# Sliding-window attention: probabilities and v in two rounded parts, v projected by features, on one Trainium2 core

## The chip, the cores and the metric

The kernel runs on one core of one Trainium2 chip. The metric is device time in microseconds. Before the change, three runs gave 2681.8, 2682.95 and 2688.42 us, with a median of 2682.95 us.

The engines are TensorE (PE, with PEld for its weight loads), VectorE (DVE), ScalarE (ACT), GpSimd (POOL) and SyncE (SP), which here only starts DMAs. Each engine works through its instructions in a fixed order, and an instruction that waits for another engine holds up everything behind it on its own engine.

## The reference

Four layers work on 16 meta tokens and 1024 sequence tokens with 1024 features. The layers are attention, mLSTM, HGRN2 and attention again. Only the two attention layers (the first and the last) matter here. They have 16 query heads in 4 groups; each group shares one key head and one value head of 64 features. A block of 128 queries sees its own block of keys and the one before it.

```python
def sliding_window_attention(q, k, v, sinks, valid):
    ...
    s = jnp.einsum('bnqhgd,bnkhd->bnhgqk', qb, kk) * (A_HD ** -0.5)
    ...
    s = jnp.where(mask[None, :, None, None], s, -jnp.inf)
    sink = sinks.astype(jnp.float32).reshape(A_KV, g, 1)
    m = jnp.maximum(s.max(axis=-1), sink)
    e = jnp.exp(s - m[..., None])
    p = e / (e.sum(axis=-1) + jnp.exp(sink - m))[..., None]
    o = jnp.einsum('bnhgqk,bnkhd->bnqhgd', p, vv)
    return o.reshape(bsz, lp, A_W)

def attention_branch(u, w_in, q_gain, k_gain, sinks, w_out, valid, pos):
    ...
    q = rope(rmsnorm(q.reshape(bsz, lp, A_HEADS, A_HD), q_gain), pos)
    k = rope(rmsnorm(k.reshape(bsz, lp, A_KV, A_HD), k_gain), pos)
    v = v.reshape(bsz, lp, A_KV, A_HD)
    o = sliding_window_attention(q, k, v, sinks, valid)
    return (o * jax.nn.silu(z.astype(jnp.float32))).astype(u.dtype) @ w_out
```

## The kernel before

**Number formats.** Everything is stored in float32. A product in F32 takes two instructions on PE, each of which passes over the moving columns. The large projections avoid this: `split` (L187) rounds an operand to F32R on ACT (the high part, suffix `h`) and takes the rest on DVE (the low part, suffix `l`), and three F32R products (high by high, high by low, low by high) are summed in PSUM, one instruction each. The profile writes both formats as f32; F32R outputs appear as fp32r.

**Layout.** The 1040 tokens are features by tokens, in three chunks of 400, 384 and 256 columns (`CHUNKS`). They form nine blocks: block 0 with the 16 meta tokens and blocks 1 to 8 with 128 each. `proj` (L238) computes 128 output features over a chunk with 24 products (L255), weights stationary. `proj_v` (L272) instead makes v with tokens as rows: for each block 24 products (L300) with u stationary and 256 value features moving. For the meta block the two parts of u lie side by side in the tile `um`, filled by GpSimd (L413), and 16 products (L296) suffice. The results go to the tiles `v`, 256 columns for all four value heads.

**The mixer.** For each of eight steps t, one PE tile of two query heads (hh = 0, 1) is processed. The blocks are grouped into units: block 0; blocks 1 and 2; 3; 4 and 5; 6; 7 and 8. For each unit there are three steps:

- `S_step` (L584): two F32R products per block give the scores in PSUM (L609, L610). POOL writes the sink beside them (L613), DVE adds the mask and finds the maximum (L614), ACT takes the exponential and its sum (L618), and DVE divides: reciprocal (L620) and a multiplication of 256 columns per block (L623).
- `T_step` (L625): PE turns the probabilities (L634, two transposes per block) into PSUM tile `pt`, and one ACT copy (L637 or L640) brings them to SBUF as `Pt`.
- `V_step` (L642): for each block two F32 products (L656), one with the previous block of v stationary and one with its own, over 128 query columns. Each product is two instructions. The stationary tile has the 128 features of two value heads, of which a query head needs 64. After the last unit of a chunk one ACT copy takes these 64 rows (L660).

In the last layer the meta block has no queries, so a layer has 96 or 80 units: 176 in all, of which 96 have two blocks, 64 have one, and 16 are the meta block.

**What sets the order.** PE's order is written by hand. `mixers` lists, for step k, the `V_step` of unit k − V_LAG, the `T_step` of unit k − T_LAG and the `S_step` of unit k, with planned costs; `weave` spreads these between the projections of the other heads in proportion to planned cost. ACT, DVE and POOL follow an order that a scheduler finds when the program is built, with raised priority for the mixer's steps. Weights arrive in halves of 128x512 through SP's queue and are split by ACT and DVE. All PSUM tiles rotate through eight buffers of one tag, v through ten, the small work tiles `t` through five.

**The stages.** The first layer's normalization and its k, v and first q projections run to 75 us; the eight steps t of the first attention layer run from there to 455 us; the mLSTM and the HGRN2 layer follow; the last attention layer has its steps t from 2252 us to the end. In t = 0, 6 and 7 there is least other work to weave in.

## Time and profile before

| | |
|---|---|
| runs | 2681.8, 2682.95, 2688.42 us |
| profiled execution: own time | 2687.3 us |
| profiled execution: span | 2685.5 us |
| mean granted TensorE clock | 0.994 |
| busy: PE, PEld, DVE, ACT, POOL | 2633.8, 2538.6, 1893.9, 1687.7, 154.2 us |

In the span's 40 equal slices, PE is at nine tenths or more in all but the first:

```profile
PE   7999999999999999999999999999999999999999
PEld 6999999999999999999999998999999899999999
DVE  6776777974747474747474688978878977677766
ACT  6767677555454545454545657877676857768673
POOL 1000000000000000000000000101000010000000
```

Slices 2 to 7 and the last seven are the attention layers. DVE and ACT are at six to eight tenths there.

### The profile page before, as it was taken

What the parts mean: (1) busy time and instruction counts of PE and PEld (TensorE: products, weight loads), DVE (VectorE), ACT (ScalarE), POOL (GpSimd) and SP (SyncE); (2) the same over time, 40 slices, a digit from 0 to 9 for tenths busy, and PEclk for the clock granted to TensorE, in tenths of its full rate; (3) what the DMA queues carried; (4) which work ended last, traced back from release to release, by engine and by line L of the source; (5) the groups of instructions that cost most, each with busy time, mean ns of one, the idle gap of its engine ahead of it and who ended that gap; (6) DMA issues with size and microseconds to landing.
All of it is one profiled execution on the core that took longest, in us unless ns stands there. A gap on an engine that the chain in (4) does not pass through costs nothing.

```text
span 2685.5 us, 55478 instructions
## 1 busy us (share of the span) xinstructions
PE 2633.8 (98%) x20896; PEld 2538.6 (95%) x20896; DVE 1893.9 (71%) x5335; ACT 1687.7 (63%) x4301; POOL 154.2 (6%) x545
## 2 busy tenths in 40 slices
PE   7999999999999999999999999999999999999999
PEld 6999999999999999999999998999999899999999
DVE  6776777974747474747474688978878977677766
ACT  6767677555454545454545657877676857768673
POOL 1000000000000000000000000101000010000000
PEclk9999999999999999999999999999999999999999
DMA  3211111011111111111111111111111111111102
GB/s 133 59 37 48 47 42 38 17 65 56 40 56 40 56 40 56 40 56 40 56 40 50 54 34 33 33 33 33 41 33 37 35 54 48 56 43 48 45 25 87
DMA packets 74044, 126.67 MB, mean 47 GB/s; under 512 B 11552, under 2 KB 26016, under 8 KB 73776
## 3 DMA queue, kind: packets, MB, share of 16 engines
q1 hardware_dynamic: 73776, 123.13, 14.4%
q8 instruction: 165, 2.70, 0.4%
q14 instruction: 103, 0.84, 0.1%
HBM read 108.24 MB, written 4.26 MB: 42 GB/s over the span
## 4 chain that ended last, share of the span: by engine, by line
PE 82%; DVE 10%; ACT 5%; DMA 1%; issue 1%; POOL 1%; SPq 0%; ACTq 0%; DVEq 0%; POOLq 0%
PE pj L255 38%; PE pj L338 15%; PE pj L300 10%; PE po L656 4%; PE pt L634 2%; PE po L862 1%; PE pm L609 1%; PE pa L532 1%; PE pa L876 1%; PE pm L610 1%; DVE t L408 1%; PE po L864 1%; DVE ul L189 1%; PE pj L296 1%; DVE x L341 1%
## 5 line engine op out<-in xcount | busy, mean ns | idle before, releaser
L255 PE MATMUL pj<-uh,wh 128*128 128x384 f32 (+2 forms) x2592 | 900.6, 347 | 3.8 <-ACT uh L188 3.8
L255 PE MATMUL pj<-ul,wh 128*128 128x384 f32 (+2 forms) x2592 | 836.5, 323 | 2.6 <-DVE ul L189 2.3
L255 PE MATMUL pj<-uh,wl 128*128 128x384 f32 (+2 forms) x2592 | 834.1, 322 | 0.1
L255 PEld LDWEIGHTS pj<-uh,wh 128*128 128x128 f32 x2592 | 492.0, 190 | 24.6 <-issue 6.6
L255 PEld LDWEIGHTS pj<-ul,wh 128*128 128x128 f32 x2592 | 492.6, 190 | 14.3 <-DVE ul L189 5.4
L255 PEld LDWEIGHTS pj<-uh,wl 128*128 128x128 f32 x2592 | 491.9, 190 | 0.4 <-DVE wl L189 0.4
L189 DVE TENSOR_TENSOR wl<-wr,wh 128x512 fp32r<-128x512 f32 x336 | 228.7, 688 | 59.6 <-ACT wh L188 56.6
L300 PE MATMUL pj<-wh,uh 128*128 128x256 f32 x896 | 270.1, 301 | 0.0
L188 ACT CAST wh<-wr 128x512 fp32r<-128x512 f32 x337 | 203.1, 618 | 96.9 <-PE pj L338 33.1
L341 DVE TENSOR_TENSOR x<-x,pj 128x384 f32<-128x384 f32 (+2 forms) x480 | 235.0, 510 | 39.7 <-PE pj L338 38.1
L338 PE MATMUL pj<-yh,wh 128*128 128x384 f32 (+2 forms) x768 | 254.0, 331 | 0.0
L300 PE MATMUL pj<-wh,ul 128*128 128x256 f32 x896 | 253.3, 283 | 0.0
L300 PE MATMUL pj<-wl,uh 128*128 128x256 f32 x896 | 253.3, 283 | 0.0
L338 PE MATMUL pj<-yl,wh 128*128 128x384 f32 (+2 forms) x768 | 246.8, 321 | 3.3 <-DVE yl L189 3.3
L338 PE MATMUL pj<-yh,wl 128*128 128x384 f32 (+2 forms) x768 | 246.0, 320 | 0.0
L428 DVE SCALAR_TENSOR_TENSOR t<-pj,t 128x384 f32<-128x384 f32 (+2 forms) x192 | 99.0, 515 | 110.4 <-ACT t L427 110.0
L618 ACT ACTIVATE Sm<-Sm,s 128x257 f32<-128x257 f32 (+2 forms) x272 | 131.7, 486 | 67.9 <-DVE s L614 65.8
L300 PEld LDWEIGHTS pj<-wl,uh 128*128 128x128 f32 x896 | 170.5, 190 | 2.2
L300 PEld LDWEIGHTS pj<-wh,uh 128*128 128x128 f32 x896 | 170.2, 190 | 2.5
L300 PEld LDWEIGHTS pj<-wh,ul 128*128 128x128 f32 x896 | 170.4, 190 | 0.0
L429 ACT ACTIVATE t<-t 128x384 f32<-128x384 f32 (+2 forms) x240 | 118.1, 492 | 81.0 <-DVE t L428 79.6
L614 DVE CUSTOM_DVE_ANT_0 Sm<-pm,masks,cons 128x256 f32<-128x256 f32 (+2 forms) x272 | 116.0, 452 | 70.0 <-PE pm L610 65.0
(218 smaller groups left out, 5290.0 us busy)
## 6 DMA issues: line engine op xcount, KB each, us to landing
wr<-in_b_win SPq DMA_DIRECT2D x128, 256.0 KB, 2.7
wr<-in_a_win SPq DMA_DIRECT2D x80, 256.0 KB, 2.7
wr<-in_c_win SPq DMA_DIRECT2D x64, 256.0 KB, 2.6
r<-rowsd SPq DMA_DIRECT2D x16, 520.0 KB, 5.8
wr<-in_a_wout SPq DMA_DIRECT2D x32, 256.0 KB, 2.7
wr<-in_b_wout SPq DMA_DIRECT2D x32, 256.0 KB, 2.7
t<-t SPq DMA_DIRECT2D x96, 48.0 KB, 1.9
wr<-in_c_wout SPq DMA_DIRECT2D x16, 256.0 KB, 2.7
```

The source lines that it names most:

```text
L188: s.copy(h, src)
L189: v.tensor_tensor(l, src, h.bitcast(F32), op=ALU.subtract)
L255: pe.matmul(acc[:, :cn], a[:, k, :], b[:, k, c0 : c0 + cn], start=(k == 0 and i == 0), stop=(k == KT - 1 and i == 2))
L300: pe.matmul(acc[:cn, :256], a[:, k, c0 : c0 + cn], m[:, kk, :], start=(k == 0 and i == 0), stop=(k == KT - 1 and i == 2))
L338: pe.matmul(acc[:, :cn], a[:, k, mc], b, start=(k == 0 and i == 0), stop=(k == 1 and i == 2))
L341: v.tensor_tensor(x[:, m, c0 : c0 + cn], x[:, m, c0 : c0 + cn], acc[:, :cn], op=ALU.add)
L428: v.scalar_tensor_tensor(a[:, :cn], z, 0.0, a[:, :cn], op0=ALU.min, op1=ALU.subtract)
L429: s.activation(a[:, :cn], a[:, :cn], AF.Exp)
L614: v.tensor_tensor_reduce(Sm[:nq, u, :nk], S[:nq, u, :nk], R["masks"][:nq, P + mo : P + mo + nk], -1.0, sink, ALU.add, ALU.min, st[:nq, u : ...
L618: s.activation(Sm[:nq, u, : nk + 1], Sm[:nq, u, : nk + 1], AF.Exp, scale=-1.0, bias=st[:nq, u : u + 1], accum_out=den[:nq, u : u + 1])
L634: pe.transpose(pt[:kn, u, ki, :nq], Sm[:nq, u, ko : ko + kn], ident[:nq, :nq])
L656: pe.matmul(po[:, q0 - c0 : q0 - c0 + nq], V[kb][:kn, gcol : gcol + P], Pt[:kn, u, ki, :nq], start=(ki == 0), stop=(ki == len(kbs) - 1))
```

## The change

The product of probabilities and v is made with F32R instead of F32.

- **v by features.** `v_proj` projects 128 value features (two value heads) with `proj`, as q and k are. The result is copied to SBUF, turned on PE (a transpose per block), and split into a high and a low part, which lie as [high head 0, low head 0, low head 1, high head 1] in 256 columns, so that 128 columns hold both parts of one head. The first two heads are projected in the head of the layer, the other two in the fill of t = 4. The meta tile `um` is no longer filled for attention layers, and has 48 columns instead of 80.
- **Probabilities in two parts.** `T_step` leaves the high part `Ph` (ACT) and the low part `Pl` (DVE). `Pl` has one buffer.
- **V_step.** Both parts pass over the stationary v of one head, [high, low] side by side, into the same 128 rows of PSUM; in a unit of two blocks the block that serves both queries is passed with 256 columns. The two halves of the rows are added: an ACT copy of one and a DVE addition of the other. V_LAG goes from 4 to 3.
- **Division.** The multiplication by the reciprocal moves from DVE to GpSimd.

```diff
-T_LAG, V_LAG = 2, 4
+T_LAG, V_LAG = 2, 3
+D_V = 1500.0
...
-                if n == 0:
-                    for z, src in ((0, uh), (64, ul)):
+                if n == 0 and self.meta:
+                    for z, src in ((0, uh), (32, ul)):
                         g.tensor_copy(um[:, k, z : z + NMETA], src[:, k, :NMETA].bitcast(F32))
...
+        def v_proj(src, jj):
+            late = {}
+            def evac(acc, n, c0, cn):
+                late[n] = tmp()
+                s.copy(late[n][:, :cn], acc[:, :cn])
+            def finish(n, c0, cn):
+                def fn():
+                    pt = psum("pt", 1)
+                    for k, b in enumerate(CHUNK_BLOCKS[n]):
+                        q0, nq = blk(b)
+                        pe.transpose(pt[:nq, P * k : P * k + P], late[n][:, q0 - c0 : q0 - c0 + nq], ident)
+                    for k, b in enumerate(CHUNK_BLOCKS[n]):
...
+                        parts = z[:nq, :256].rearrange("p (a c) -> p a c", a=4)
+                        src = pt[:nq, P * k : P * k + P].rearrange("p (a c) -> p a c", a=2)
+                        s.copy(parts[:, 0:4:3], src)
+                        v.tensor_tensor(parts[:, 1:3], src, parts[:, 0:4:3].bitcast(F32), op=ALU.subtract)
...
+            return proj(src, evac), [finish(n, *c) for n, c in enumerate(CHUNKS)]
...
-                    v.tensor_scalar(Sm[:nq, u, :nk], Sm[:nq, u, :nk], den[:nq, u : u + 1], None, op0=ALU.mult)
+                    g.tensor_scalar(Sm[:nq, u, :nk], Sm[:nq, u, :nk], den[:nq, u : u + 1], None, op0=ALU.mult)
...
-                w["Pt"] = Pt = R["mix"].tile([P, 2, 2, P], F32, tag="Pt", name=nm("Pt"), bufs=2)
+                w["Ph"] = Ph = R["mix"].tile([P, 2, 2, P], F32R, tag="Ph", name=nm("Ph"), bufs=2)
+                w["Pl"] = Pl = R["mix"].tile([P, 2, 2, P], F32R, tag="Pl", name=nm("Pl"), bufs=1)
...
+                s.copy(h, src)
+                v.tensor_tensor(l, src, h.bitcast(F32), op=ALU.subtract)
...
+                    runs = [(b, P, P * (2 * k + 1), 2 * P if k + 1 < len(unit) else P, P * k) for k, b in enumerate(unit)]
+                    runs.insert(1, (b0 - 1, P, 0, P, 0))
+                for i, (kb, kn, p0, w_, q0) in enumerate(runs):
+                    for part in ("Ph", "Pl"):
+                        flat_p = w[part].rearrange("p u k q -> p (u k q)")
+                        pe.matmul(po[:, a0 + q0 : a0 + q0 + w_], V[t // 4, kb][:kn, P * hh : P * hh + P],
+                                  flat_p[:kn, p0 : p0 + w_], start=(i == 0 and part == "Ph"),
+                                  stop=(i == len(runs) - 1 and part == "Pl"))
                 if w["last"]:
...
+                    s.copy(o, po[hs, :cn])
+                    v.tensor_tensor(o, o, po[os, :cn], op=ALU.add)
...
-                for lag, cost, fn in ((V_LAG, 427, V_step), (T_LAG, 213, T_step), (0, 218, S_step)):
+                for lag, cost, fn in ((V_LAG, 260, V_step), (T_LAG, 213, T_step), (0, 218, S_step)):
...
-        vg = proj_v(win[2], win[3], v_evac)
+        vg0, vfin0 = v_proj(win[2], 0)
+        vg1, vfin1 = v_proj(win[3], 1)
...
+            if t == 4:
+                parts.append(tile_of(vg1, vfin1))
```

The instructions of PE around one unit, in the first attention layer at t = 7, blocks 4 and 5, hh = 0. Before, its transposes and what follows at once (Sm holds the probabilities, pt their transposes, pm the scores of a later unit, po the output, pj a projection):

```order
L656 MATMUL po_5356<-Pt_5414,v_423 128x128
L634 MATMUL pt_5494<-const,Sm_5429 128x128 x4
L609 MATMUL pm_5501<-r_2857,qs_5107 128x256
L610 MATMUL pm_5501<-kl_2858,qs_5107 128x256
L656 MATMUL po_5383<-Pt_5456,v_381 128x128
L656 MATMUL po_5383<-Pt_5456,v_423 128x128
L255 MATMUL pj_5515<-uh,wh_5041 128x256
```

After these come five more projection products, and then the next unit's transposes and scores ahead of this unit's own products with v, which read Pt_5495:

```order
L634 MATMUL pt_5522<-const,Sm_5461 128x128 x4
L609 MATMUL pm_5529<-r_2859,qs_5110 128x256
L610 MATMUL pm_5529<-kl_2860,qs_5110 128x256
L656 MATMUL po_5540<-Pt_5495,v_423 128x128
L656 MATMUL po_5540<-Pt_5495,v_523 128x128 x2
L656 MATMUL po_5540<-Pt_5495,v_573 128x128
```

With the change, the same unit's transposes (L660) are followed by two score products (L634, L635) and then at once by its own products with v (L687):

```order
L687 MATMUL po_5716<-Pl_5832,v_3499 128x128
L660 MATMUL pt_5874<-const,Sm_5802 128x128 x4
L634 MATMUL pm_5883<-r_2879,qs_5449 128x256
L635 MATMUL pm_5883<-kl_2880,qs_5449 128x256
L687 MATMUL po_5894<-Ph_5875,v_3581 128x256
L687 MATMUL po_5894<-Pl_5876,v_3581 128x256
L687 MATMUL po_5894<-Ph_5875,v_3502 128x128
L687 MATMUL po_5894<-Pl_5876,v_3502 128x128
L687 MATMUL po_5894<-Ph_5875,v_3584 128x128
L687 MATMUL po_5894<-Pl_5876,v_3584 128x128
```

What moved: the transposes and the products that use them had the other unit's work and six projection products between them; now they have two score products. The eight instructions of the product (four F32 products of two) are six.

On DVE near the same place, before (ISA is the masked maximum and the reading of its result):

```order
L620 RECIPROCAL s_5463<-s_5463 128x2
L623 TENSOR_SCALAR Sm_5461<-Sm_5461,s_5463 128x256 x2
L614 ISA Sm_5502,s_5503<-pm_5501,masks_220,cons_222 128x256
L614 ISA s_5503 128x1
L620 RECIPROCAL s_5504<-s_5504 128x1
L623 TENSOR_SCALAR Sm_5502<-Sm_5502,s_5504 128x256
```

and with the change:

```order
L645 RECIPROCAL s_5840<-s_5840 128x2
L639 ISA Sm_5884,s_5885<-pm_5883,masks_194,cons_196 128x256
L639 ISA s_5885 128x1
L694 TENSOR_TENSOR r_5675<-r_5675,po_5716 64x400
L666 TENSOR_TENSOR Pl_5876<-pt_5874,Ph_5875 128x512
L645 RECIPROCAL s_5886<-s_5886 128x1
```

The multiplications are gone. The low part of the probabilities stands behind the next masked maximum and behind the addition that ends the chunk of another unit.

On POOL at the beginning of the mixer, with the change (before, only the L613 copies stood here, now L638):

```order
L638 COPY Sm_689<-cons_196 16x1
L638 COPY Sm_707<-cons_196 16x1
L648 ISA
L648 TENSOR_SCALAR Sm_689<-Sm_689,s_691 16x16
L638 COPY Sm_730<-cons_196 128x1 x2
L648 TENSOR_SCALAR Sm_707<-Sm_707,s_709 16x16
L638 COPY Sm_791<-cons_196 128x1 x2
L648 TENSOR_SCALAR Sm_730<-Sm_730,s_732 128x144
L648 TENSOR_SCALAR Sm_730<-Sm_730,s_732 128x256
```

The sink copy of a later unit now stands behind or ahead of the multiplications, which wait for DVE's reciprocals; one ISA instruction stands ahead of the first multiplication.

More of the change, by code (lines that the diff above doesn't have):

```diff
@@ L166, in hybrid_kernel @@
     ul = cpool.tile([P, KT, T], F32R, name="ul")
-    um = cpool.tile([P, KT, 80], F32R, name="um")
+    um = cpool.tile([P, KT, 48], F32R, name="um")
     g.memset(um.bitcast(F32), 0.0)
@@ L634, in T_step @@
                         pe.transpose(pt[:kn, u, ki, :nq], Sm[:nq, u, ko : ko + kn], ident[:nq, :nq])
[L635 to L640 removed]
+                if unit[0] == 0:
+                    src, h, l = (z[:NMETA, 0, 0, :nq] for z in (pt, Ph, Pl))
+                else:
+                    src, h, l = (z[:, :nu] for z in (pt, Ph, Pl))
+                s.copy(h, src)
+                v.tensor_tensor(l, src, h.bitcast(F32), op=ALU.subtract)
             def V_step(w):
[L643 removed]
+                unit, geo, hh, n, t = w["unit"], w["geo"], w["hh"], w["n"], w["t"]
                 nq = blk(unit[0])[1]
```

52 lines of the change are left out of this document (24 added, 28 removed).

## The prediction

> **What bounds the kernel now.** I read the page first, then the stretches of 20 us, then who waits for whom.
>
> ```profile
> span 2685.5 us, 55478 instructions
> PE 2633.8 (98%) x20896; PEld 2538.6 (95%) x20896; DVE 1893.9 (71%) x5335; ACT 1687.7 (63%) x4301; POOL 154.2 (6%) x545
> ...
> PE 82%; DVE 10%; ACT 5%; DMA 1%; issue 1%; POOL 1%; SPq 0%; ACTq 0%; DVEq 0%; POOLq 0%
> ```
>
> PE is busy for 98% of the span and makes 82% of the chain that ended last. The change touches only the two attention layers, so I look there. The columns are the stretch, its length, the busy time and count of PE, PEld, DVE, ACT and POOL, then granted clock and DMA:
>
> ```profile
> 320.00:340.00 20.00, 20.00 (x150) 19.51 (x149) 12.71 (x41) 10.48 (x29) 2.30 (x8) 1.00 0.19 59
> ...
> 400.00:420.00 20.00, 20.00 (x154) 19.48 (x152) 15.13 (x54) 16.82 (x49) 2.05 (x10) 1.00 0.01 2
> 420.00:440.00 20.00, 19.14 (x147) 18.38 (x146) 13.07 (x53) 16.19 (x47) 2.07 (x12) 1.00 0.01 2
> ```
>
> PE has hardly any idle time even in t = 7 (414 to 455 us), where ACT is busy for 16.8 of 20 us. PE's waits in the mixer are few, and those for the operands of L656 are nearly none:
>
> ```profile
> PE pt L634 <- DVE Sm L623: 3.1, 4, 1.4
> ...
> PE po L656 <- ACT v L270: 0.7, 1, 0.7
> ```
>
> So PE's order is the bound: work taken from PE is time gained, and each new wait on PE is time lost.
>
> **Products with v.** Starts of successive instructions give their price.
>
> ```profile
> 103.61 0.28 PE L255 MATMUL pj<-uh,wh 128*128 128x256 f32 x1
> 103.73 0.28 PE L255 MATMUL pj<-ul,wh 128*128 128x256 f32 x1
> ...
> 104.31 1.05 PE L656 MATMUL po<-Pt,v 128*128 128x128 f32 x8
> ...
> 69.14 2.85 PE pj L300 x24
> ...
> L656 PE MATMUL po<-Pt,v 128*128 128x128 f32 x1024 | 140.8, 275 | 0.7 <-ACT v L270 0.7
> L634 PE MATMUL pt<-const,Sm 128*128 128x128 f32 x512 | 82.5, 273 | 3.9 <-DVE Sm L623 3.1 <-ACT r L660 0.8
> ```
>
> An F32R product over 256 columns takes 0.119 us: two start 0.12 us apart, and 24 in the chain of waits take 2.85 us. An F32 instruction over 128 columns takes (1.05 − 0.275)/7 = 0.111 us. Before: 1024 × 0.111 = 113.7 us. After: the 96 units of two blocks have two products over 256 columns each, 192 × 0.119 = 22.8 us, and all 160 units have four over 128 columns, 640 in all. With p us for one of those, PE saves 90.9 − 640p. No row shows an F32R product over 128 columns. Half of the 256-column one is p = 0.06; the F32 product over the same columns is two instructions, p = 0.222. Between them lies the weight load, since every product here loads its own 128 columns:
>
> ```profile
> 83.21 0.29 PEld L656 LDWEIGHTS po<-Pt,v 16*128 16x128 f32 x2
> 83.22 0.39 PE L656 MATMUL po<-Pt,v 16*128 16x16 f32 x2
> ...
> L656 PE MATMUL po<-Pt,v x1056: 257/275/377, 83.2 to 2633.9; 128*128 128x128 f32 x171, 16*128 16x16 f32 x5
> L609 PEld LDWEIGHTS pm<-r,qs x272: 93/188/329, 75.2 to 2621.7; 128*128 128x128 f32 x128, 128*16 128x16 f32 x8
> ```
>
> Two products of only 16 moving columns still start 0.39 − 0.257 = 0.13 us apart, and their loads 0.29 − 0.19 = 0.10 us. An F32R load takes 188 ns for 128 columns and 93 for 16: the load, not the width, sets the pace of a narrow product. I take p = 0.111, nearest to the rows with 128 weights; 0.10 to 0.13 would save 27 to 8 us. **PE saves 19.9 us**, all of it in the units of two blocks; a unit of one block keeps four instructions of the same price.
>
> The Trainium skill, page "TensorE: Matmul & The Clock Gate", section "Back-to-back issue gap", speaks for more: it measured 81 ns for pairs of load and product at 128 columns. By it PE would save 39 us, and the forecast below would become 2678 us; the pair above, 0.10 to 0.13 us apart, does not agree with it.
>
> **v by features.** Before, 16 + 192 products over 256 columns a layer: 416 × 0.119 = 49.5 us in both.
>
> ```profile
> 108.25 0.34 PE L255 MATMUL pj<-uh,wh 128*128 128x400 f32 x1
> 108.43 0.34 PE L255 MATMUL pj<-ul,wh 128*128 128x400 f32 x1
> 108.61 0.35 PE L255 MATMUL pj<-uh,wl 128*128 128x400 f32 x1
> ...
> 108.80 0.60 PE L634 MATMUL pt<-const,Sm 128*128 128x128 f32 x4
> ...
> 109.77 0.58 ACT L640 COPY Pt<-pt 128x512 f32<-128x512 f32 x1
> ```
>
> After, 96 products in each chunk: 0.18 us for 400 columns, 0.173 in proportion for 384, and 0.119, so 96 × 0.472 = 45.3 us, and 36 transposes at (0.60 − 0.273)/3 = 0.109 us, 3.9 us. **Sum −0.3 us.** Half the projection, 12 us, leaves the head of the first layer, where PE is not always the bound, for t = 4, where it is:
>
> ```profile
> 40.00:50.00 10.00, 8.66 (x55) 7.69 (x55) 9.42 (x21) 8.79 (x22) 0.00 (x0) 1.00 0.08 21
> 50.00:60.00 10.00, 9.80 (x70) 8.49 (x69) 8.07 (x20) 6.96 (x19) 0.00 (x0) 1.00 0.01 2
> 60.00:70.00 10.00, 10.00 (x58) 9.65 (x58) 4.56 (x11) 8.84 (x20) 0.00 (x0) 1.00 0.29 86
> ```
>
> From 60 us on PE alone is full, so removing work there shortens the head; around 45 us DVE is (9.4 of 10), and PE could idle. The products that waited for `um` there are gone too. I set this term to 0, between −3 and +9 us.
>
> **The new wait.** This is the term that decides. Before, between a unit's last transpose and its first product with v lay more than a whole round of other work; with V_LAG 3 there is less than one, and now two steps must fit in instead of one: the ACT copy `Ph`, then DVE's `Pl`.
>
> ```profile
> L640 ACT COPY Pt<-pt 128x512 f32<-128x512 f32 x96 | 56.0, 583 | 13.2 <-PE pt L634 11.4 <-PE pm L610 0.8
> L640 ACT COPY Pt<-pt 128x256 f32<-128x256 f32 x64 | 23.5, 366 | 11.8 <-PE pt L634 11.5
> L189 DVE TENSOR_TENSOR wl<-wr,wh 128x512 fp32r<-128x512 f32 x336 | 228.7, 688 | 59.6 <-ACT wh L188 56.6
> L189 DVE TENSOR_TENSOR ul<-t,uh 128x256 fp32r<-128x256 f32 x32 | 13.1, 421 | 0.8 <-ACT uh L188 0.6
> ```
>
> With nothing in the way, a unit of two blocks needs, after its last transpose's turn on PE, 0.16 us until that transpose ends (0.273 − 0.109), 0.58 for the copy, 0.69 for the low part and 0.12 for the handovers: 1.56 us. (The 0.12 is an estimate: here DVE starts 0.03 us after ACT's end, which comes twice, and PE has to begin again.)
>
> ```profile
> 100.54 0.55 ACT L355 ACTIVATE t<-t 128x400 f32<-128x400 f32 x1
> ...
> 101.12 0.57 DVE L540 TENSOR_TENSOR t<-t,t 128x400 f32<-128x400 f32 x1 [0.98 <-ACT t L355]
> ```
>
> A unit of one block needs 0.16 + 0.37 + 0.42 + 0.12 = 1.08 us. In the place shown in the change, two score products stand between, 0.24 us: PE must wait for 1.3 us, and behind that product everything on PE waits too: transposes and scores of the next units and the projection.
>
> I priced the products between, with the numbers above, for all 160 units of the changed order. Of them 40 have less than 1.5 us and 88 less than 2 us; in the order before, none has less than 2 us. The shortfalls sum to 19 us if nothing is queued before the two steps. Something is: the copies started 0.37 us after the last transpose's end in the row above (108.80 + 0.60 to 109.77), and here 0.22 us:
>
> ```profile
> 105.92 0.38 PE L634 MATMUL pt<-const,Sm 128*128 128x128 f32 x2
> ...
> 106.52 0.37 ACT L640 COPY Pt<-pt 128x256 f32<-128x256 f32 x1
> ```
>
> With 0.3 us of queueing for both engines together the shortfalls sum to 34.5 us, with 0.6 us to 55, with 0.9 us to 83. I take 0.3 us, near the smaller of the two, since a PE that waits lets ACT and DVE catch up: **+34.5 us**, most of it in t = 0, 5, 6 and 7 of the first layer and t = 7 of the last.
>
> **DVE, ACT and POOL.** DVE loses the multiplications and gains the low parts and the closing additions.
>
> ```profile
> L623 DVE TENSOR_SCALAR Sm<-Sm,s 128x256 f32<-128x256 f32 x224 | 73.3, 351 | 3.0
> L613 POOL COPY Sm<-cons x272: 175/186/1304, 25.2 to 2621.9; 128x1 f32<-128x1 f32 x128, 16x1 f32<-16x1 f32 x8
> L613 POOL COPY Sm<-cons 128x1 f32<-128x1 f32 x256 | 57.4, 249 | 734.0 <-PE pt L634 362.4 <-ACT Sm L618 72.1 <-ACT t L355 32.4
> L1135 POOL COPY att<-rd 32x64 f32<-32x64 f32 x128 | 53.9, 421 | 507.2 <-DVE rd L1133 501.7
> ```
>
> The low parts are 96 × 0.69 + 64 × 0.42 = 93 us, about what the multiplications took, so DVE keeps its 13 to 15 of 20 us, with some 50 us more for 96 closing additions (0.5 us each, an estimate from the 0.42 and 0.69 above) over the 830 us of both layers. POOL's multiplication over 256 columns has no row. Its copies take 0.19 us for one column and 0.42 for 64, so it lies between DVE's 0.35 and, with 3.6 ns a column, 1.1 us; I take 0.45. That is 0.1 us a block and a handover longer than before, in a path from scores to transposes that has two rounds and gains two waits of PE: I cost it at nothing. If POOL takes 1.1 us, it adds about 1.5 us a unit to that path, and the dense units wait for it. The ISA row in front of it has no price in the trace; it stands behind copies that ran from 25.2 us on, and the first scores come at 75.2 us, so 50 us cover it.
>
> A rule speaks against this move: by the Trainium skill, page "SBUF — State Buffer", section "SBUF: two separate sides", GpSimd and a DVE instruction with two SBUF inputs exclude each other for a whole instruction. The longest sink copy above, 1304 ns against a median of 186, agrees. If each of the 256 long multiplications lost what the mean of those copies is above their median (249 − 186 ns), all of it on PE's path, the sum would be 16 us higher.
>
> **Sum.** 2687.3 (the profiled execution's own time) − 19.9 − 0.3 + 0 + 34.5 = 2701.6 us. The median of the runs, 2682.95, lies 4.35 us below that execution, so I forecast 2697 us.
>
> **Rivals.**
> - *Narrow products run at their width* (p = 0.06). For it: wide F32R products cost in proportion to columns. Against it: the pair of 16 columns. PE saves 52.5 us instead of 19.9: 2664 us, faster. It beats the waits of 34.5 us from p below 0.088.
> - *The F32R product over 128 columns is as slow as F32* (p = 0.222): the halving does not happen. No row excludes it. PE loses 51 us: 2768 us.
> - *The two steps are not late*: shortfalls between 0 and the floor of 19 us, because the scheduler places them first. 2663 to 2682 us. Against it: L694 and L639 stand ahead of L666 in DVE's order.
> - *Everything on ACT, DVE and POOL queues up* (0.9 us a unit, ACT being at 16.8 of 20): 2745 us.
>
> **How the numbers follow.** A measurement of this kernel can tell about 0.3% (8 us) from no change. Forecast 0.48 (own range 2680 to 2722: slower 0.38, same 0.10); products at their width 0.17 (faster 0.13, same 0.04); as slow as F32 0.12 (slower); steps not late 0.13 (faster 0.07, same 0.06); queueing 0.10 (slower). Faster 0.20, same 0.20, slower 0.60. The range from 2661 to 2756 leaves out the F32 case and the ends of the others.
>
> **What would show it.** The spacing of the narrow L687 rows gives p. L687 should appear among PE's waits for DVE `Pl`, with some 30 us, and PE's idle time in t = 0, 6 and 7 should rise from nearly 0 to 1 to 2 us in 20. The transposes L660 should not wait for POOL more than L634 waited for DVE. The first scores should come some 10 us earlier than 75.2 us. The forecast is wrong if p is far from 0.111, or if L687 hardly waits.

## The result, and the profile after

| | before | after |
|---|---|---|
| median of the runs | 2682.38 us (2679.79 to 2688.42, 4 runs) | 2755.64 us (2754.68 to 2759.61, 4 runs) |
| profiled execution, own time | 2687.3 us | 2759.6 us |
| ratio | | 1.0269, 95% interval 1.0251 to 1.0287 |

The kernel became 73 us slower. The forecast was 14 us slower.

The page of the changed kernel, with the rows that answer to those of before (span, busy time, the slices of PE and of POOL, the chain of work that ended last):

```profile
span 2757.8 us, 55198 instructions
...
PE 2649.7 (96%) x20612; PEld 2532.5 (92%) x20612; DVE 1968.0 (71%) x5369; ACT 1693.9 (61%) x4331; POOL 379.2 (14%) x787
...
PE   6899998999999999999999999999999998999999
...
POOL 0433244100000000000000000101000102332340
...
PE 70%; DVE 14%; ACT 8%; DMA 3%; issue 3%; POOL 1%; SPq 1%; DVEq 0%; ACTq 0%; POOLq 0%
```

PE's share of the chain falls from 82% to 70%, DVE's and ACT's rise from 15 to 22% together. PE's idle time, span less busy time, rises from 51.7 to 108.1 us. PE has 284 instructions fewer, yet 16 us more busy time: a product that starts after a pause is shown longer, as the rows of one unit will show, and work at half the clock, some 14 us more than before by the table below, counts as busy. A stretch of t = 6 in the first layer now (the columns are those of the stretches above):

```profile
420.00:440.00 20.00, 17.71 (x119) 16.14 (x118) 16.59 (x47) 14.85 (x42) 9.21 (x17) 1.00 0.12 34
```

Before, PE had no idle time in t = 6; now it has 2.3 of 20 us, with DVE at 16.6. Who PE waits for (total us, times, longest):

```profile
PE po L687 <- DVE Pl L666: 30.9, 53, 2.1
...
PE po L687 <- ACT Ph L665: 13.3, 23, 1.7
...
PE pt L660 <- POOL Sm L648: 5.5, 8, 1.3
```

The wait is where the prediction put it. Its size has to be read from starts, since this view counts only time in which PE was empty. For each pair of neighbouring PE instructions (line and form of both) I took the lower quartile of the time from start to start, over the traces of all runs shown here. The sum of these is called *work*. What a spacing has beyond it, if over 40 ns, is *lost*: to the instruction that came late, or to *half clock* where it began in a stretch of half the granted clock without idle time ahead. In us of each profiled execution:

| | work | of it P·v | lost at products with v | lost at transposes | half clock | all else | first to last PE start |
|---|---|---|---|---|---|---|---|
| before | 2460.0 | 114.9 | 2.7 | 5.4 | 14.6 | 190.3 | 2673.0 |
| after | 2444.6 | 96.5 | 78.6 | 6.4 | 28.9 | 186.5 | 2745.0 |
| difference | −15.4 | −18.4 | +75.9 | +1.0 | +14.3 | −3.8 | +72.0 |

The price of a narrow product with v in this count is 0.11 us. In the changed kernel 130 of the 640 started only 0.06 us after the one ahead, most of them the second narrow product behind wide ones, so PE saved some 7 us more than the 18.4; the count has that under "all else". The 79 us are in 192 places, spread over the dense stages: 6.5, 7.0, 6.0, 6.3 and 9.7 us in t = 0, 1, 5, 6, 7 of the first layer, 8.7 and 9.9 in t = 3 and 7 of the last.

One unit of t = 5 shows how. First PE, then ACT, then DVE in the timeline (start, duration, engine, line, operation, and in brackets the idle time ahead and who ended it):

```profile
380.73 0.60 PE L660 MATMUL pt<-const,Sm 128*128 128x128 f32 x4
...
382.34 0.28 PE L635 MATMUL pm<-kl,qs 128*128 128x256 f32 x1
383.13 0.38 PE L687 MATMUL po<-Ph,v 128*128 128x256 f32 x1 [0.51 <-ACT Ph L665]
383.86 0.38 PE L687 MATMUL po<-Pl,v 128*128 128x256 f32 x1 [0.34 <-DVE Pl L666]
384.08 0.22 PE L687 MATMUL po<-Ph,v 128*128 128x128 f32 x1
384.14 0.27 PE L687 MATMUL po<-Pl,v 128*128 128x128 f32 x1
384.25 0.27 PE L687 MATMUL po<-Ph,v 128*128 128x128 f32 x1
...
381.58 0.49 ACT L693 COPY r<-po 64x400 f32<-64x400 f32 x1
382.10 0.50 ACT L427 ACTIVATE t<-pj 128x400 f32<-128x400 f32 x1
382.50 0.58 ACT L665 CAST Ph<-pt 128x512 fp32r<-128x512 f32 x1
...
383.11 0.69 DVE L666 TENSOR_TENSOR Pl<-pt,Ph 128x512 fp32r<-128x512 f32 x1 [0.44 <-ACT Ph L665]
```

The transposes end at 381.33, but `Ph` begins at 382.50: ACT first takes another unit's closing copy and a piece of the gate. PE comes to the product at about 382.46 (382.34 and the usual 0.12), and starts it at 383.13. Then it waits for `Pl` too. The two products start 0.73 us apart, and the next one 0.22 us later, where without a wait each takes 0.12. PE loses 0.67 + 0.61 + 0.10 = 1.4 us here, of which the view of waits counts 0.85.

### The profile page after: what moved, and what is told of

The parts are those of the page before. It is cut to its first block, busy times and chain, and to the rows that moved or that the text cites. A ratio compares the mean times of both kernels' runs of the same rounds, so it can differ in the third digit from the quotient of the medians.

```text
span 2757.8 us, 55198 instructions
## 1 busy us (share of the span) xinstructions
PE 2649.7 (96%) x20612; PEld 2532.5 (92%) x20612; DVE 1968.0 (71%) x5369; ACT 1693.9 (61%) x4331; POOL 379.2 (14%) x787
## 4 chain that ended last, share of the span: by engine, by line
PE 70%; DVE 14%; ACT 8%; DMA 3%; issue 3%; POOL 1%; SPq 1%; DVEq 0%; ACTq 0%; POOLq 0%
PE pj L256 33%; PE pj L339 14%; PE pj L301 9%; PE po L687 2%; ACT Sm L643 1%; DMA t<-t 1%; PE pt L660 1%; DVE Pl L666 1%; PE po L901 1%; DVE t L410 1%; PE pa L915 1%; DVE ul L190 1%; PE po L903 1%; SPq L526 1%; DVE wl L190 1%
## 5 line engine op out<-in xcount | busy, mean ns | idle before, releaser
L256 PE MATMUL pj<-uh,wh 128*128 128x384 f32 (+2 forms) x2688 | 932.9, 347 | 4.6 <-ACT uh L189 4.6
L256 PE MATMUL pj<-ul,wh 128*128 128x384 f32 (+2 forms) x2688 | 870.9, 324 | 3.6 <-DVE ul L190 3.5
L256 PE MATMUL pj<-uh,wl 128*128 128x384 f32 (+2 forms) x2688 | 868.2, 323 | 0.0
L256 PEld LDWEIGHTS pj<-ul,wh 128*128 128x128 f32 x2688 | 513.7, 191 | 14.8 <-DVE ul L190 6.6
L648 POOL TENSOR_SCALAR Sm<-Sm,s 128x256 f32<-128x256 f32 (+2 forms) x272 | 252.4, 937 | 523.3 <-DVE s L645 509.4
L339 PE MATMUL pj<-yh,wh 128*128 128x384 f32 (+2 forms) x768 | 252.2, 328 | 0.0
L339 PE MATMUL pj<-yl,wh 128*128 128x384 f32 (+2 forms) x768 | 246.9, 321 | 3.2 <-DVE yl L190 3.2
L339 PE MATMUL pj<-yh,wl 128*128 128x384 f32 (+2 forms) x768 | 246.0, 320 | 0.0
L301 PE MATMUL pj<-wh,uh 128*128 128x256 f32 x768 | 231.3, 301 | 0.0
L301 PE MATMUL pj<-wh,ul 128*128 128x256 f32 x768 | 216.6, 282 | 0.0
L301 PE MATMUL pj<-wl,uh 128*128 128x256 f32 x768 | 216.5, 282 | 0.0
L189 ACT CAST yh<-r 128x384 fp32r<-128x384 f32 (+2 forms) x120 | 57.2, 479 | 152.1 <-PE pj L339 130.6
L339 PEld LDWEIGHTS pj<-yl,wh 128*128 128x128 f32 x768 | 144.7, 188 | 5.8 <-DVE yl L190 5.2
L301 PEld LDWEIGHTS pj<-wh,uh 128*128 128x128 f32 x768 | 145.2, 189 | 2.1
```

Of the source, the lines that this page charges most:

```text
L189: s.copy(h, src)
L256: pe.matmul(acc[:, :cn], a[:, k, :], b[:, k, c0 : c0 + cn], start=(k == 0 and i == 0), stop=(k == KT - 1 and i == 2))
L301: pe.matmul(acc[:cn, :256], a[:, k, c0 : c0 + cn], m[:, kk, :], start=(k == 0 and i == 0), stop=(k == KT - 1 and i == 2))
L339: pe.matmul(acc[:, :cn], a[:, k, mc], b, start=(k == 0 and i == 0), stop=(k == 1 and i == 2))
L648: g.tensor_scalar(Sm[:nq, u, :nk], Sm[:nq, u, :nk], den[:nq, u : u + 1], None, op0=ALU.mult)
```

## The experiments

Lost times are those of the table above, worked out in the same way from each run's trace. P·v stands for the products with v.

The column of half clock varies by itself: in the mLSTM and HGRN2 layers, where nothing was changed, it is between 6 and 17 us over these executions, so a difference of a few us in it tells nothing of an edit.

| run | median us | ratio to before (95%) | lost at P·v | at transposes | half clock |
|---|---|---|---|---|---|
| the change | 2755.6 | 1.0269 (1.0251 to 1.0287) | 78.6 | 6.4 | 28.9 |
| e1_control | 2800.3 | 1.0443 (1.0428 to 1.0459) | 76.7 | 6.4 | 30.6 |
| e1_lag4 | 2764.0 | 1.0308 (1.0292 to 1.0323) | 5.2 | 40.3 | 27.2 |
| e2_high_only | 2723.7 | 1.0158 (1.0141 to 1.0175) | 48.6 | 8.7 | 22.6 |
| e2_high_only_lag4 | 2701.1 | 1.0074 (1.0059 to 1.0089) | 5.0 | 32.4 | 16.5 |
| e3_mul_dve | 2759.2 | 1.0278 (1.0263 to 1.0293) | 83.7 | 2.8 | 25.0 |
| e3_high_only_lag4_mul_dve | 2696.1 | 1.0039 (1.0024 to 1.0055) | 5.4 | 20.1 | 20.0 |
| e4_order | 2721.2 | 1.0136 (1.0121 to 1.0151) | 18.9 | 32.8 | 20.3 |
| e4_order_mul_dve | 2708.1 | 1.0082 (1.0067 to 1.0097) | 31.6 | 9.4 | 16.0 |
| e5_before_mul_pool | 2694.0 | 1.0047 (1.0032 to 1.0062) | 2.3 | 18.7 | 10.2 |
| e5_order_mixed | 2717.2 | 1.0134 (1.0112 to 1.0156) | 31.4 | 11.8 | 24.9 |
| e5_scores_first_mul_dve | 2709.9 | 1.0109 (1.0093 to 1.0125) | 35.9 | 7.2 | 20.3 |
| e5_scores_first_mixed | 2716.3 | 1.0129 (1.0110 to 1.0148) | 34.1 | 11.9 | 22.8 |
| e6_close_later | 2754.7 | 1.0282 (1.0267 to 1.0297) | 76.4 | 5.8 | 33.4 |
| e6_no_addition | 2744.3 | 1.0239 (1.0223 to 1.0254) | 67.2 | 6.7 | 21.5 |
| e6_order_close_later | 2710.7 | 1.0113 (1.0098 to 1.0128) | 33.5 | 6.0 | 20.1 |
| e6_order_two_buffers | 2728.8 | 1.0179 (1.0162 to 1.0196) | 6.8 | 32.4 | 26.5 |
| e7_fill_in_t7 | 2696.3 | 1.0056 (1.0042 to 1.0070) | 28.7 | 3.8 | 12.8 |
| e7_fill_in_t6 | 2704.9 | 1.0086 (1.0073 to 1.0098) | 26.5 | 7.5 | 22.2 |

### More distance between transposes and products

```diff
-ROWS, TMPS, RAWS, YS, QS = 9, 5, 2, 3, 6
+ROWS, TMPS, RAWS, YS, QS = 9, 5, 2, 2, 6
-T_LAG, V_LAG = 2, 3
+T_LAG, V_LAG = 2, 4
-tag="Pl", name=nm("Pl"), bufs=1
+tag="Pl", name=nm("Pl"), bufs=2
```

> The changed kernel with V_LAG 4 and two buffers for Pl; to make room, the small tiles yh and yl of the output projection get two buffers instead of three (the control beside it has this alone). Theory Q (a product with v comes too soon after its transposes: the order leaves 40 of 160 units less than 1.5 us, while the copy Ph and the low part Pl need 1.1 to 1.6 us plus 0.84 us of queueing): in the new order no unit has less than 2 us, so L687's lost time falls from 99 to under 8 us and the time to 2655 to 2675 us. Rival P (the multiplication on POOL, 1.01 us a block, sets the pace of the mixer): the transposes wait for POOL in place of the products, and the time stays at 2700 to 2740 us. Rival D (DVE and ACT have too much work in the dense stages whatever the order): 2700 us or more, with the wait still at L687.

The control has the first edit (YS 2) alone.

> The changed kernel with two instead of three buffers for yh and yl, and nothing else. If the third buffer does not matter: 2747 to 2764 us, waits as in the changed kernel. If the output projection needs it, the time rises, L339 waits, and the kernel with V_LAG 4 carries the same loss.

The control shows that the third buffer was needed: going without it costs 45 us, lost at the output projection (L339). PE's wait there in the control:

```profile
PE pj L339 <- DVE yl L190: 20.2, 42, 2.0
```

So the pair has to be compared with itself. With V_LAG 4 and the second buffer for `Pl` the time is 36 us lower than in the control, and the products no longer lose anything worth naming. But the transposes do. PE's waits with V_LAG 4:

```profile
PE pt L660 <- POOL Sm L648: 27.7, 42, 2.1
...
PE po L687 <- DVE Pl L666: 0.3, 1, 0.3
```

Theory Q is right about the place (77 us lost there become 5), rival P about what comes next: the transposes take 34 of the 72 us back, mostly waiting for POOL's multiplication.

### One step instead of two

```diff
-                s.copy(h, src)
-                v.tensor_tensor(l, src, h.bitcast(F32), op=ALU.subtract)
+                s.copy(h, src)
...
-                        flat_p = w[part].rearrange("p u k q -> p (u k q)")
+                        flat_p = w["Ph"].rearrange("p u k q -> p (u k q)")
```

> The changed kernel without the low part of the probabilities: DVE's L666 is left out and the products that read Pl read Ph again, so PE does the same work in the same order (V_LAG 3) and waits for one step instead of two. Theory Q: with one step and some 0.5 us of queueing the shortfalls of the order sum to 15 to 20 us instead of 76 to 99, so 2675 to 2695 us. Rival P (POOL): 2735 us or more, since nothing changes on POOL. Rival A (it is the copy on ACT that is late, DVE's step hides behind it): L687 still loses 60 us or more, 2715 us or more.

> The same without the low part, with V_LAG 4: one step and no unit with less than 2 us. L687 should lose nothing, so this shows what PE's work itself has become: by the spacing of the products in the changed kernel's trace PE saves 32 us of instruction time, and with the head 5 us earlier the time is 2645 to 2660 us. If POOL's multiplication bounds the mixer the transposes L660 wait and it is 2680 us or more.

Without the low part the products still lose 49 us, far from the 15 to 20 of theory Q and nearer to rival A: the copy on ACT is often late by itself. With V_LAG 4 beside it they lose 5, and the transposes 32, the most of it behind POOL. PE's waits, first with V_LAG 3 (here the product is L685, the copy L664 and the transpose L659):

```profile
PE po L685 <- ACT Ph L664: 30.8, 34, 2.5
...
PE pt L659 <- POOL Sm L648: 7.2, 12, 1.3
```

and with V_LAG 4:

```profile
PE pt L659 <- POOL Sm L648: 22.4, 38, 1.4
```

### The multiplication

```diff
-                    g.tensor_scalar(Sm[:nq, u, :nk], Sm[:nq, u, :nk], den[:nq, u : u + 1], None, op0=ALU.mult)
+                    v.tensor_scalar(Sm[:nq, u, :nk], Sm[:nq, u, :nk], den[:nq, u : u + 1], None, op0=ALU.mult)
```

> The changed kernel with the multiplication by the reciprocal back on DVE, everything else as changed (V_LAG 3, one buffer for Pl). Theory Q2 (two things come one after the other: with V_LAG 3 the products with v wait for Ph and Pl and lose 77 us; POOL's multiplications are hidden behind these waits and cost 30 to 40 us only when they are gone): within 20 us of the changed kernel, 2735 to 2775 us, L687 still the place of the loss. Rival P (POOL is the cause already now): 2715 us or less.

> Without the low part of the probabilities (products read Ph twice), V_LAG 4, and the multiplication on DVE. Without the last of the three, 2701 us were measured, with 32 us lost at the transposes. Theory Q2: DVE has room here, the transposes lose less than 8 us and the time is 2665 to 2680 us, faster than before the change. Rival S (the path from scores to transposes is late whoever multiplies, for instance by the exponential on ACT): the transposes still lose 20 us or more, 2690 us or more.

In the changed kernel it makes no difference who multiplies: 2759 against 2756 us. Where the products do not wait, the transposes lose 20 instead of 32 us; that is rival S's result, not the less than 8 us of theory Q2. The path from scores to transposes is too long for these rounds even with DVE multiplying.

The opposite edit, in the kernel before:

> The kernel before the change with one part of the change alone: the multiplication by the reciprocal on POOL instead of DVE. Theory Q2 (POOL's 0.92 us a block is hidden in the changed kernel only because the products with v already wait): here nothing else waits, so the transposes wait for POOL, 20 to 35 us, and the time is 2700 to 2720 us. Rival H (rounds before the change are longer and hide POOL): within 8 us of 2683 us.

It costs 12.9 us, between the two cases. PE's waits there:

```profile
PE pt L634 <- POOL Sm L623: 13.8, 23, 1.7
```

Before the change this wait was 3.1 us, for DVE. What a multiplication takes on POOL, in the changed kernel's groups of instructions (busy us, mean ns of one):

```profile
L648 POOL TENSOR_SCALAR Sm<-Sm,s 128x256 f32<-128x256 f32 x224 | 225.0, 1012 | 305.8 <-DVE s L645 293.7 <-PE pm L635 6.3 <-PE pt L660 5.4
L648 POOL TENSOR_SCALAR Sm<-Sm,s 128x144 f32<-128x144 f32 x32 | 22.0, 688 | 144.6 <-DVE s L645 142.8 <-PE pt L660 1.7
```

### Another order of the three steps

```diff
-                for lag, cost, fn in ((V_LAG, 260, V_step), (T_LAG, 213, T_step), (0, 218, S_step)):
+                for lag, cost, fn in ((T_LAG, 213, T_step), (0, 218, S_step), (V_LAG, 260, V_step)):
```

> The changed kernel with the three steps of a round in another order: transposes, scores, then the products with v, instead of the products first; V_LAG 3, one buffer for Pl, nothing else changed. In this order a unit has at least 2.05 us of other work between its transposes and its products (40 units had less than 1.5 us), and no memory is needed. Theory Q2: L687 loses 5 to 20 us instead of 77, the transposes 30 to 45 us instead of 6, and the time is 2705 to 2730 us. Rival B (one buffer for Pl now bounds, since the low part can start only when the products of the unit before are done): L687 still loses 40 us or more, 2735 us or more.

> The same order, with the multiplication on DVE too. Theory Q2: neither the products nor the transposes wait much, 2670 to 2690 us, about as before the change or a little faster. Rival D (DVE, with multiplications, low parts and closing additions all on it, becomes late): waits for Pl and for Sm of 30 us or more in the dense stages, 2705 us or more.

This order needs no memory and takes 34 us off the changed kernel, as theory Q2 said: 19 us lost at the products, 33 at the transposes. PE's waits:

```profile
PE pt L660 <- POOL Sm L648: 23.7, 35, 1.6
PE po L687 <- DVE Pl L666: 9.8, 16, 1.3
```

With DVE multiplying, the loss at the transposes falls to 9, but that at the products rises to 32:

```profile
PE po L687 <- DVE Pl L666: 18.1, 26, 1.5
...
PE pt L660 <- DVE Sm L648: 6.5, 12, 1.2
```

Rival D holds here. Two more edits, sharing the multiplication and starting the scores first, do no better:

```diff
-                    g.tensor_scalar(Sm[:nq, u, :nk], Sm[:nq, u, :nk], den[:nq, u : u + 1], None, op0=ALU.mult)
+                    (v, g)[u].tensor_scalar(Sm[:nq, u, :nk], Sm[:nq, u, :nk], den[:nq, u : u + 1], None, op0=ALU.mult)
...
-                for lag, cost, fn in ((T_LAG, 213, T_step), (0, 218, S_step), (V_LAG, 260, V_step)):
+                for lag, cost, fn in ((0, 218, S_step), (T_LAG, 213, T_step), (V_LAG, 260, V_step)):
```

> The changed kernel in the order transposes, scores, products, and with the multiplication shared: the first block of a unit on DVE, the second on POOL at the same time. With all of it on POOL 2721 us (33 us lost at the transposes, 19 at the products), with all of it on DVE 2708 us (9 and 32). Theory Q2 with a DVE that is nearly full in the dense stages: the path to the transposes has the length that DVE alone gives it or little more and DVE is 28 us freer, 2695 to 2708 us. Rival: POOL's part sets the pace of the two-block units, 2710 us or more.

> The changed kernel in the order scores, transposes, products, with the multiplication on DVE. Scores start some 0.5 us earlier relative to their transposes and a product comes 0.5 us sooner after them. If the path from scores to transposes is what is short in the dense stages: 2695 to 2705 us. If DVE's load is (18 of 20 us there): 2705 to 2712 us, as in the other order.

> The same order with the multiplication shared between DVE and POOL as in the run above. If both the path and DVE's load count, this is the fastest of the four: 2685 to 2700 us. If neither is what is left, 2705 us or more.

Scores first with DVE multiplying gives 2710 us, the case of DVE's load. The mixed runs, 2717 and 2716 us, gained nothing over these, against both forecasts of a gain: POOL does not hold the transposes there (12 us lost), yet the loss at the products stays at 31 to 34 us although DVE has less to do, and half clock takes 23 to 25 us. Why, these runs don't show.

### What holds the rest: closing steps, a buffer, or the load

`hi` is the raised priority of the mixer's steps; `close` holds the closing copy and addition, taken out of `V_step`:

```diff
-                        step = [cost * len(w["unit"]), hi(lambda w=w, fn=fn: fn(w)), None]
+                        def both(w=w, fn=fn):
+                            hi(lambda: fn(w))()
+                            if fn is V_step and w["last"]:
+                                close(w)
+                        step = [cost * len(w["unit"]), both, None]
```

`e6_order_close_later` is the same on top of `e4_order_mul_dve`. `e6_no_addition` leaves out one line, and `e6_order_two_buffers` changes three numbers on top of `e4_order_mul_dve`:

```diff
-                    v.tensor_tensor(o, o, po[os, :cn], op=ALU.add)
...
-ROWS, TMPS, RAWS, YS, QS = 9, 5, 2, 3, 6
+ROWS, TMPS, RAWS, YS, QS = 9, 5, 2, 3, 5
-bufs=12 if w < 8 else 4
+bufs=8 if w < 8 else 4
-tag="Pl", name=nm("Pl"), bufs=1
+tag="Pl", name=nm("Pl"), bufs=2
```

> The changed kernel with the closing copy (L693) and the closing addition (L694) scheduled without the raised priority that the mixer's steps have, so that Ph and Pl of the next unit need not stand behind them; V_LAG 3 and all else unchanged. In the changed kernel's trace the 104 units whose product waited for Pl had 0.60 us of other ACT work ahead of Ph and 0.40 us of other DVE work ahead of Pl; the closing steps are 14 of 62 us of the one and 9 of 40 us of the other. Theory C (the closing steps, new with the change, make the queue): the products lose 55 to 62 us instead of 79, 2732 to 2742 us. Rival L (it is the load as a whole; other work moves up into the place): within 8 us of the changed kernel.

> The changed kernel with the closing addition left out (the output keeps only the half of the rows that the copy takes); the 50 us of DVE work are gone. Theory C: 2735 to 2745 us, as with the closing steps later or somewhat more. Theory L: each us of DVE work ahead counts, but only 9 us of it stands ahead of a late Pl, so 2740 to 2750 us. If DVE's load does not matter at all: 2750 to 2760 us.

> The order transposes, scores, products with the multiplication on DVE (2708 us measured, 32 us lost at the products), and the closing steps without raised priority. Theory C: the loss at the products falls by 8 to 15 us, 2693 to 2700 us. Theory L: 2700 to 2712 us.

> The order transposes, scores, products with the multiplication on DVE and two buffers for Pl; to make room the tiles qs of the queries get five buffers instead of six and the smallest tiles eight instead of twelve. Rival B (with one buffer the low part can start only when the products of the unit before are done, and this holds the products): their loss falls from 32 to under 12 us, 2685 to 2695 us if the fewer buffers elsewhere cost nothing. Theory L (in the trace a late Pl stood 2.1 us behind other DVE work after the buffer was free): the loss stays above 20 us, 2700 us or more.

Without the raised priority nothing changes (2754.7 and 2710.7 us), but this does not decide on theory C, because the edit hardly moved the closing steps. In the trace of `e6_close_later`, 41 closing copies and 24 closing additions still stand ahead of late units, with 15.5 and 8.7 us; in the changed kernel it is 39 and 25, with 14.3 and 8.8 us. On top of `e4_order_mul_dve` it is the same: 27 copies and 20 additions, against 29 and 17 without the edit. What speaks against theory C is their share: together they are 23 us of the 104 us that the late units of the changed kernel spent between their transposes, `Ph` and `Pl`. Leaving 49 us of additions out gives 11 us, by the ratios 8, about what stood ahead of late units; both theories had allowed that. The second buffer for `Pl` does what rival B says at the products (32 become 7) and yet the transposes lose 32 instead of 9, and the statistics of q (L534) wait some more:

```profile
PE pt L660 <- DVE Sm L648: 18.8, 24, 1.9
...
PE pa L534 <- ACT t L523: 7.9, 7, 2.5
```

The loss moves between the two places and does not go. That the second buffer for `Pl` is what moved it is not shown: the run also has fewer buffers for `qs` and for the smallest tiles, which hold the maxima and sums on the path from scores to transposes, and no run has these alone. The last two runs changed neither place, but gave PE more of its own work in a dense stage (`e7_fill_in_t7` on top of `e4_order_mul_dve`; `e7_fill_in_t6` moves the same work to t = 6):

```diff
-            if t in (2, 4):
+            if t == 2:
...
-            if t % 2 or t == 6:
+            if t in (1, 3, 4, 5, 6, 7):
...
+            if t == 7:
+                splits, products = outs(oc[3])
+                parts.append((products, [(-Y_AHEAD, z) for z in splits]))
```

> The order transposes, scores, products with the multiplication on DVE (2708 us), and one more thing moved: the output projection of heads t = 2 and 3 (about 22 us of PE work, with its splits and additions) from the fill of t = 4, which now also has the second projection of v, to that of t = 7, which has least. Theory L (in the dense stages ACT, DVE and POOL need longer for a round than PE, and work of PE's own is the only cover): the 13 us that products and transposes lose in the two stages t = 7 fall to 3 or less, 2694 to 2702 us. Rival M (the splits and additions that go with it load ACT and DVE there as much as they cover): 2704 to 2712 us.

> The same, moved to t = 6, where products and transposes lose 8 us in the two layers together. Theory L: 2699 to 2705 us, a smaller gain than in t = 7. Rival M: 2704 to 2712 us.

Three stretches of t = 7 without the moved work:

```profile
424.00:434.00 10.00, 8.10 (x47) 7.56 (x47) 8.15 (x32) 7.04 (x24) 0.78 (x5) 0.83 0.00 1
434.00:444.00 10.00, 10.00 (x71) 9.26 (x70) 9.19 (x34) 7.38 (x22) 1.09 (x6) 1.00 0.01 2
444.00:454.00 10.00, 8.41 (x66) 7.70 (x65) 9.27 (x29) 9.38 (x26) 1.64 (x6) 1.00 0.16 55
```

and with it:

```profile
424.00:434.00 10.00, 10.00 (x67) 9.88 (x67) 9.02 (x28) 4.93 (x15) 0.79 (x5) 1.00 0.01 2
434.00:444.00 10.00, 10.00 (x74) 9.93 (x72) 9.76 (x27) 5.16 (x14) 0.48 (x3) 1.00 0.16 53
444.00:454.00 10.00, 10.00 (x75) 9.88 (x74) 8.72 (x27) 6.02 (x17) 0.38 (x2) 1.00 0.35 107
```

PE is full, DVE as busy as before. In the two stages t = 7 products, transposes and half clock lose 1.5 us instead of 14.8, and 1.4 of it are at one product of the last units. Stages t = 4 and 5 of the first layer, which have less cover now, lose 4.0 us more. The span is 11.4 us shorter, the median 12 us; measured by the ratios, each against its own runs of the kernel before, it is 7 us, and the intervals touch. In t = 6 the same move gains less, and by the ratios nothing that can be told.

No version here is faster than the kernel before. The best version of the changed kernel with the full computation is `e7_fill_in_t7`, 0.56% slower.

## Why the prediction had the right sign and the wrong size

**Price of the products: right, a little too high.** The price was 0.111 us. PE's work on P·v fell by 18.4 us at 0.11 us for every narrow product, or by some 25 us with those 130 that took 0.06; forecast 19.9, within 8 to 27. In the unit above the weight loads of the narrow products start 0.11 us apart (384.08, 384.19, 384.30) and the products with them (384.14, 384.25, 384.36); only the second narrow one, behind the wide ones, comes 0.06 us after the one ahead (384.08 to 384.14). So the load set the pace, as the prediction said. As prices of all narrow products both rivals, at width and as slow as F32, are out; the first holds for a fifth of them.

**v by features: right.** Work of projections and transposes changed by −0.5 us, forecast −0.3. The first scores came 5.6 us earlier (69.6 instead of 75.2 us), not 10; no run looked into that.

**The new wait: right place, size too small, and this is the step that failed.** I took 0.3 us of queueing for ACT and DVE together, "since a PE that waits lets ACT and DVE catch up". In the trace 104 of 160 units were late: their first product with `Pl` started within 0.4 us of `Pl`'s end. Between their last transpose's end and `Ph` lay 0.60 us, between `Ph` and `Pl` 0.40 us; ACT was busy with other work for 0.54 us of the first, DVE for 0.36 us of the second. They did not catch up, since they had work of their own. So the queue was 1.0 us in the late units, and 0.84 us (0.48 for ACT, 0.36 for DVE) over all 160: that of the rival "queues up" (0.9 us, 83 us by its sum), which had got a chance of 0.10. So 75.9 us more were lost at the products instead of 34.5. That the order sets this wait is shown by `e1_lag4`: with more distance and a second buffer for `Pl` it is gone, and 72 us lost at this place with it. ACT's part could have been read beforehand: in the trace of before, the copies of `Pt` began 0.50 us after the last transpose's end on average over the 16 stages (0.15 to 1.34 us). I used two rows of 0.22 and 0.37 us instead, and nothing for DVE. With 0.50 us the sum, between the prediction's 34.5 us for 0.3 and 55 for 0.6, would still have been only some 48 us, an estimate: DVE's part had no row before the change.

**Half clock: missing from the sum.** It costs 14.3 us more than before in the profiled execution, some 5 us of it before 70 us and the rest in and just behind the attention stages. With both terms as measured, the sum would be 2687.3 − 19.9 − 0.3 + 75.9 + 14.3 = 2757.3 us; the profiled execution took 2759.6. Both terms come from that execution's trace, so the sum shows that little is left over, and no more. The median lies 0.4 us inside the stated range (2661 to 2756) only because the range reached over the rival "queues up" (2745 us).

**POOL at nothing: right for this kernel, for the wrong reason.** The transposes lost 1.0 us more. I costed it at nothing because of the room in two rounds. `e1_lag4` and `e4_order` show that the room is not there: as soon as the products do not wait, the transposes lose 33 to 40 us. The multiplication took 1.01 us on average, not 0.45, near the upper bound of 1.1. The 16 us that I worked out beside the Trainium skill's page "SBUF — State Buffer", section "SBUF: two separate sides", are not borne out: `e3_mul_dve`, without these multiplications on POOL, is not faster, and the DVE instructions that both kernels have took only 4.2 us longer in all with the multiplications on POOL. The rule itself shows in part of the rows: DVE's instructions of two SBUF tiles at 128x384 (L541) took 647 ns where they overlapped a multiplication on POOL (13 of them) and 552 ns elsewhere (15), but those of L540, of the same shape, 564 (11) and 551 ns (17); `Pl`, which has one input in PSUM, 689 and 688 ns at 128x512.

**Why nothing brought the gain back.** Most of the runs fit one mechanism, which is argued and not shown. Before the change ACT and DVE were already busy for 16.8 and 15.1 of the 20 us from 400 us on, most of which is t = 6 (the prediction took it for t = 7, where ACT has 16.2). The change shortens PE's round and adds to the others `Pl` (95.6 us), the closing additions (49.1 us) and POOL's slower multiplication. Then PE waits somewhere. V_LAG, order, buffers and the multiplying engine decide whether at the products or at the transposes; together these lose 32 to 52 us in all the versions with another order (before: 8), and that is 24 to 44 us more, above the 15 us of work saved, or some 22 with the 130 narrow products at 0.06 us. Only `e7_fill_in_t7` and, weakly, `e7_fill_in_t6` took something away, by giving PE other work. More work on PE also puts more time between the steps of a unit, so these two runs do not tell whether the load of the other engines or the length of a unit's path is what is short; the mixed runs, where DVE had less to do and nothing was gained, do not fit the load alone. Whether the sum of all dense stages can be brought under the work saved in this way was not tried: t = 0, 1, 5 and 6 still lose in `e7_fill_in_t7`.

## What to carry to other kernels

Before taking work from the engine that bounds a stage, add up what the others need for the same round, and how long one unit's path through them is; where these are close, the gain can end there and not at zero waits. Where a step is put between two instructions of an in-order engine, price the queue ahead of it by the mean that the same kind of handover already shows in that stage, for each engine in the path, and not by the best rows; for a step that is new, as `Pl` on DVE was here (0.36 us), allow a queue too. The order of the steps within a round is a lever that costs no memory: here it gave 34 us.

## What the hardware showed beside this

**The clock.** In the changed kernel the granted clock halved for 18 stretches of 3.41 us or twice that, before for 9 (a last piece at the span's end included). Their starts lie on a grid of 3.41 us. Two such stretches with the one ahead of each, the columns as above:

```profile
442.29:445.70 3.41, 1.55 (x13) 1.24 (x12) 2.64 (x8) 2.44 (x8) 2.26 (x4) 1.00 0.00 0
445.70:449.11 3.41, 2.77 (x13) 2.49 (x11) 1.03 (x5) 1.03 (x4) 0.17 (x1) 0.50 0.00 0
469.60:473.01 3.41, 1.82 (x13) 1.63 (x14) 2.57 (x7) 3.27 (x8) 2.75 (x3) 1.00 0.47 154
473.01:476.42 3.41, 3.41 (x19) 3.41 (x17) 2.30 (x5) 1.36 (x4) 0.39 (x1) 0.50 0.00 0
```

PE was empty for 1.9 and 1.6 us of the stretch ahead; over the 18 it was 1.0 to 2.9 us. Other stretches of 3.41 us with 1.0 to 1.8 us without work on PE were not followed by half clock; in this kernel all with more were. In the second pair PE is full at half clock, so the pause is paid twice. The Trainium skill, page "TensorE: Matmul & The Clock Gate", section "What's actually happening", has the free-running window of 3413 ns, and the trace agrees with it. The same section of the Trainium skill has the clock drop after an idle window of that length. Here pauses of a third to most of it were enough. That fits the Trainium skill, same page, section "A second HAM failure mode: psum-queue depth-cycling", where many short pauses do the same.

**Starting again.** After a wait the next two products start 0.22 us apart where 0.12 is usual (383.86 to 384.08 above). The waits view leaves this out, and also the time for which the product ahead of the wait is still shown as running (in the unit above 0.67 us are lost at the wait for `Ph`, of which it shows 0.51). It shows 47.7 us at L687 (30.9, 13.3, and 3.5 in two smaller rows), the starts 78.6.

**POOL.** A multiplication by a column of scalars takes 0.69 us for 144 columns and 1.01 for 256 on POOL, on average, against 0.35 us on DVE for the latter.
